# Seven half products per pair of tiles: products with unsummed weights a pair ahead, convolution taps and pooling sums one operation behind each product

## The chip, the core and the metric

The kernel runs on one core of one Trainium2 chip. The metric is the device time of one execution in microseconds (us). The engines are named as in the profile: PE (TensorE, matmuls; PEld its weight loads), DVE (VectorE), ACT (ScalarE), POOL (GpSimd) and SP (SyncE, which issues most DMAs). Each engine works through its own instructions in a fixed order and waits at each for what it needs from the others.

## The reference

One inference step of a small decoder trunk: a Mamba-2 (SSD) layer and a causal pooling layer, on 1024 prompt tokens and 8 x 8 sample tokens, 1088 in all, with width 1024. Cut to what this case touches:

```
zxbcdt = h @ w_in                                     # SSD layer: 1024 -> 2048 z + 4096 xbc + 32 dt
conv = conv_b + sum(xp[:, k:k + L] * conv_w[k] for k in range(4))
xbc_act = silu(conv);  B, C, xs = split of xbc_act;  y = scan over chunks of 128
out = rmsnorm_by_group(y * silu(z)) @ w_out

uz = h @ w_in                                         # pooling layer: 1024 -> 2048 u + 2048 z
win_sum = cs[off:off + L] - cs[off - w:off - w + L]   # windows 2, 4, 8, 16, by channel group
pooled = win_sum / min(w, pos + 1) - u
out = (pooled @ w_group * ch_scale * silu(z)) @ w_out
```

All arithmetic is float32. On PE each product is made of three terms of reduced precision: weights and activations are split into a high and a low half, and hi x hi, hi x lo and lo x hi are added up.

## The kernel before, in words

Channels lie on the 128 partitions and tokens along the free axis. An input projection takes a weight of 128 output channels (8 blocks of 128 inputs) and gives one output tile of 128 x 1088. The program runs through these stages: a start; twelve *front pairs* of output tiles of the SSD projection (`front_pairs`, from `FRONT`: z2 z3 z4 b5 x5 z5 b7 x7 z6 b0 x0 z7, where b and x tiles go through the convolution and z tiles through a SiLU); the scan with the other projections beside it; the output projection of the SSD layer; the input projection of the pooling layer, two pairs plainly and 14 *pooling pairs* (`fast_pairs`, p = 2 to 15, each a u tile, which is pooled, and a z tile); the group products; the output projection; the last norm.

The change touches the front pairs and the pooling pairs. Both go through `fast_run`. With the weights u and z of a pair of output tiles, each in two halves over the inputs (f and l), and the activations in halves over inputs and tokens (B11, B21, B22, and sums T1 to T4 made beforehand), the two tiles come from seven half products instead of eight. Each is named by the activations that it takes. One half product (`product`) is 24 matmuls of 128 x 272: two chunks of tokens, four blocks of inputs, three terms. Its results stay in two PSUM banks; some products add to what an earlier one left there. ACT copies banks out (`copy`, L1012; L1056 for the half tile that is not summed), DVE adds a bank to an earlier copy and writes the output (`put`, L1009).

The weights of the seven products are made by `w_sums`: POOL adds and subtracts raw halves (L948, L949, L951, L953), then `split_half` makes a high half on ACT (L174) and a low half on DVE or, for two of seven, on POOL (L176). A product's weight is made three products ahead. The halves lie in a ring of four tiles, so the high half of a product can only start when the product four before it is done. Raw weights (`wr`, 512 KB each) come by DMA in a ring of three, sums (`sw`) in a ring of two.

Behind a pair's last product (B22), `after("B22")` issues what the finished tiles need: in the front `proj_end`, which calls `conv_tile` (per tile: copies of the new convolution state on POOL, the first tap on ACT, L351, three taps for prompt and sample each on DVE, L349, then a SiLU on ACT, L352), in the pooling stage `u_pool` (state copies on POOL, L838 and L839; doublings of the window sum on DVE, L845; a correction, L850; and the difference, L852 and L854). A scheduler then sets the fixed order of every engine from the order in which the program issues the work and from its own estimates.

Of the kernel before, what the change touches and what calls it, by code (L numbers as in the profile page):

```python
# [28 lines left out]
POOLW = (3, 5)  # L29
# [68 lines left out]
class Build:  # L98
# [69 lines left out]
    def split_half(self, src):  # L168

        n = self.nsplit  # L170
        self.nsplit += 1
        t = self.wp.tile([P, 8, P], F32R, tag=("wh", "wl")[n % 2], bufs=2, name=self.name("w"))
        hi, lo = t[:, 0:4, :], t[:, 4:8, :]
        self.nc.scalar.activation(hi, src, AF.Copy)  # L174
        eng = self.nc.gpsimd if n % 7 in POOLW else self.nc.vector
        eng.tensor_tensor(out=lo, in0=src, in1=hi.bitcast(F32), op=ALU.subtract)  # L176
        return hi, lo
# [158 lines left out]
    def conv_tile(self, ti, raw, dst, ncv, scan):  # L336
# [6 lines left out]
        if not scan:  # L343
            w = [self.vec[:, V_CW + 4 * ti + k:V_CW + 4 * ti + k + 1] for k in range(4)]
            sd = dst[:, NP:TOK].rearrange("p (b i) -> p b i", i=8)
            for k in range(4):
                for d, r in ((dst[:, :NP], raw[:, k:k + NP]), (sd, rv[:, :, k:k + 8])):
                    if k:
                        nc.vector.scalar_tensor_tensor(out=d, in0=r, scalar=w[k], in1=d, op0=ALU.mult, op1=ALU.add)  # L349
                    else:  # L350
                        nc.scalar.activation(d, r, AF.Identity, bias=self.vec[:, V_CB + ti:V_CB + ti + 1], scale=w[0])  # L351
            nc.scalar.activation(dst, dst, AF.Silu)  # L352
            return
# [26 lines left out]
    def proj_end(self, G, ii, raw, scan=False):  # L380
        dst = self.slots.get("xbc")
        self.conv_tile(G["ti"][ii], raw, dst, G["ncv"][:, ii], scan)
# [33 lines left out]
    def proj_evict(self, G, ii, raw, ps, c):  # L416
# [3 lines left out]
        if pn < n:  # L420
            nc.scalar.activation(raw[:, 1027:1115].rearrange("p (b w) -> p b w", w=11)[:, :, 3:11],
                                 ps[:, pn:n].rearrange("p (b i) -> p b i", i=8), AF.Identity)
            self.proj_end(G, ii, raw, True)
# [409 lines left out]
    def u_pool(self, p, U):  # L833
# [8 lines left out]
        while step < w:  # L842
# [5 lines left out]
            s, step = d, 2 * step  # L848
        o = 16 - w
# [86 lines left out]
    def w_sums(self, n):  # L936
# [4 lines left out]
        u = self.stream_next_raw()  # L941
        self.stream_raw(self.wpos)
        yield self.split_half(u[:, f])
        for i in range(n):
            z = self.stream_next_raw()
            self.stream_raw(self.wpos)
            s = self.tp.tile([P, 8, P], F32, tag="sw", bufs=2, name=self.name("sw"))
            nc.gpsimd.tensor_tensor(out=s[:, f], in0=z[:, f], in1=z[:, l], op=ALU.add)  # L948
            nc.gpsimd.tensor_tensor(out=s[:, l], in0=s[:, f], in1=u[:, f], op=ALU.subtract)  # L949
            yield self.split_half(s[:, l])  # L950
            nc.gpsimd.tensor_tensor(out=z[:, f], in0=u[:, f], in1=z[:, f], op=ALU.subtract)  # L951
            yield self.split_half(z[:, f])
            nc.gpsimd.tensor_tensor(out=s[:, l], in0=u[:, l], in1=s[:, l], op=ALU.subtract)  # L953
            yield self.split_half(u[:, l])
            yield self.split_half(s[:, f])
            if i + 1 < n:
                u = self.stream_next_raw()
                self.stream_raw(self.wpos)
                yield self.split_half(u[:, f])
            yield self.split_half(z[:, l])  # L960
            yield self.split_half(s[:, l])

    def fast_init(self, n):

        self.nsplit = 0
# [8 lines left out]
    def product(self, ps, x, more=False):  # L974
# [10 lines left out]
        for c in range(2):  # L985
            t = slice(QUART * c, QUART * c + QUART)
            for k, (xh, xl) in enumerate(self.X[x]):
                nc.tensor.matmul(ps[c], hi[:, k], xh[:, t], start=(k == 0 and not more), stop=False, skip_group_check=True)  # L988
                nc.tensor.matmul(ps[c], hi[:, k], xl[:, t], start=False, stop=False, skip_group_check=True)  # L989
                nc.tensor.matmul(ps[c], lo[:, k], xh[:, t], start=False, stop=(k == 3), skip_group_check=True)  # L990

    def fast_run(self, n, make):
# [21 lines left out]
        def first(i):  # L1014
            A = banks(*(("y", "y"), ("mm", "mm"))[i % 2])
            product(A, "B11")
            s = self.tp.tile([P, HALF], F32, tag="mt2", bufs=self.nmt2, name=self.name("m1"))
            for c in range(2):
                copy(s[:, cs[c]], A[c])
            return A, s  # L1020

        A, s = first(0)
        for i in range(n):
            u, z, after = make(i)
            after("B11")
# [5 lines left out]
            E = banks("mm", "S")  # L1031
            product(E, "T3")
            v = self.tp.tile([P, HALF], F32, tag="mt2", bufs=self.nmt2, name=self.name("m7"))
            for c in range(2):
                copy(v[:, cs[c]], E[c])
            after("T3")
            B = banks("tr", "tr")
            product(B, "B21")
            for c in range(2):
                put(u, 0, c, B[c], s[:, cs[c]])  # L1040
            after("B21")
# [5 lines left out]
            nxt = first(i + 1) if i + 1 < n else None  # L1047
            product(E, "T4", True)
            for c in range(2):
                put(z, 0, c, E[c], z1[:, cs[c]])  # L1050
                after(f"z0{c}")
            after("T4")
            product(A, "B22", True)
            for c in range(2):
                for o, w in parts(u, 1, c):
                    nc.scalar.activation(o, w(A[c]), u[3])  # L1056
            after("B22")
            if nxt:
                A, s = nxt

    def fast_pairs(self, late):
# [5 lines left out]
        def make(i):  # L1067
# [3 lines left out]
            def after(x):  # L1071
# [11 lines left out]
                elif x == "B22":  # L1083
                    if p - PLAIN < len(late):
                        self.u_pool(p - PLAIN, late[p - PLAIN])
                    if p < 15:
                        self.u_pool(p, U)
# [3 lines left out]

        self.fast_run(16 - PLAIN, make)
        self.free_acts(self.hn[4:])
# [347 lines left out]
    def front_pairs(self, ops, dt):  # L1441
# [4 lines left out]

        def make(n):
# [11 lines left out]
            def after(x):  # L1459
# [9 lines left out]
                if kind != "z" and x == "B22":  # L1469
                    for i in range(2):  # L1470
                        self.proj_end(G, ii + i, ts[i])
                        if g:
                            t = G["out"].pop()
                            nc.sync.dma_start(self.xbd[g][ii + i], t)
                            sl.free(t)
                if n == 0 and x in ("B11", "T2"):
# [13 lines left out]
        self.fast_run(len(FRONT), make)  # L1490
        sl.free(*[self.T[4, k] for k in range(4)])
# [115 lines left out]
    def pool_layer(self):  # L1607
# [28 lines left out]
        for gi in range(4):  # L1636
            acts, zs = self.group_split(gi > 0), self.gin[1]
            if gi == 0:
                self.u_pool(15, U)
# [202 lines left out]
```

## Time and profile before

| | |
|---|---|
| median of 3 runs | 1648.8 us (1647.14 to 1650.06) |
| profiled execution | 1648.84 us, span 1647.1 us |
| PE busy | 1602.4 us (97%) |
| DVE busy | 1208.0 us (73%) |
| ACT busy | 860.7 us (52%) |
| POOL busy | 482.0 us (29%) |
| front pairs | 96.6 to 369 us of the span |
| pooling pairs | 1069 to 1369.4 us of the span |

In rows of the profile a group is written as line, engine, operation, output<-inputs, shapes and count; then busy time and the mean of one in ns; then the idle time of the engine just before them and who ended it. `st` is a bank of a half product, `w` a split weight, `hh`, `hl` and `t` activations, `xbc` a tile behind the convolution, `raw` one ahead of it, `u`, `ws` and `pl` the tile, its window sums and its pooled result, `pz` a z tile of the pooling layer. Rows of the timeline start with the start in us from the span's start and the duration in us; a row with x9 stands for nine instructions in a row of which the first has the shape shown. Rows of windows give the stretch, its length, the busy time (and count) of the engines, then the granted clock of PE, the DMA share and GB/s.

### The profile page before, as it was taken

How to read it: one execution, taken by the hardware profiler on the slowest of the kernel's cores; microseconds unless marked ns; L12 is line 12 of the kernel's file. 1: busy time of each engine (PE TensorE's matmuls, PEld its weight loads, DVE VectorE, ACT ScalarE, POOL GpSimd, SP SyncE). 2: the span in 40 equal slices, each digit the busy share in tenths (PEclk: the TensorE clock that was granted, in tenths of full speed). 3: DMA queues.
4: the chain of work that ended last, by engine and by line, in shares of the span. 5: the costliest groups of instructions: out<-in, count | busy, mean ns of one | idle time of the engine just before them, and what ended most of it. 6: DMA issues, size and time to landing. Idle time of an engine off the chain costs nothing.

```text
span 1647.1 us, 30656 instructions
## 1 busy us (share of the span) xinstructions
PE 1602.4 (97%) x12061; PEld 1525.9 (93%) x12061; DVE 1208.0 (73%) x1912; ACT 860.7 (52%) x1735; POOL 482.0 (29%) x527
## 2 busy tenths in 40 slices
PE   8999999999999999999999999999999999999997
PEld 6899999999888998898989899999999999999997
DVE  6863657576787878889878867966777647577886
ACT  6663445457766676675545536644333344233364
POOL 0224444331212212020211212455565640000241
PEclk9999999999999999999999999999999999999999
DMA  9422332235545555578788633033233359655783
GB/s 343 161 73 92 106 109 81 87 131 186 176 144 192 162 163 164 186 230 295 277 326 302 219 127 118 29 110 125 104 98 110 128 169 369 214 154 179 161 177 116
DMA packets 122305, 275.59 MB, mean 167 GB/s; under 512 B 18192, under 2 KB 59312, under 8 KB 122160
## 3 DMA queue, kind: packets, MB, share of 16 engines
q1 hardware_dynamic: 118128, 260.91, 45.9%
q0 software_dynamic: 4032, 12.72, 4.4%
q8 instruction: 95, 1.56, 0.4%
q14 instruction: 50, 0.41, 0.1%
HBM read 201.12 MB, written 70.23 MB: 165 GB/s over the span
## 4 chain that ended last, share of the span: by engine, by line
PE 74%; DVE 9%; DMA 5%; issue 4%; POOL 4%; ACT 3%; SPq 0%; DVEq 0%; POOLq 0%; ACTq 0%
PE mm L182 10%; PE mm L183 9%; PE mm L184 9%; PE st L990 9%; PE st L988 9%; PE st L989 9%; DVE xbc L349 3%; PE op L1229 2%; PE op L1230 2%; PE op L1228 2%; DMA acb<-acd 2%; PE y L609 2%; PE S L588 2%; PE y L613 1%; PE am L253 1%
## 5 line engine op out<-in xcount | busy, mean ns | idle before, releaser
L990 PE MATMUL st<-hh,w 128*128 128x272 f32 x832 | 243.3, 292 | 13.3 <-DVE w L176 11.8
L988 PE MATMUL st<-hh,w 128*128 128x272 f32 x832 | 241.8, 291 | 2.4 <-ACT pz L862 2.4
L989 PE MATMUL st<-hl,w 128*128 128x272 f32 x832 | 241.8, 291 | 0.0
L990 PE MATMUL st<-t,w 128*128 128x272 f32 x624 | 179.6, 288 | 0.0
L988 PE MATMUL st<-t,w 128*128 128x272 f32 x624 | 179.5, 288 | 0.0
L989 PE MATMUL st<-t,w 128*128 128x272 f32 x624 | 179.2, 287 | 0.0
L182 PE MATMUL mm<-hh,wh 128*128 128x368 f32 (+1 forms) x528 | 178.1, 337 | 0.1
L184 PE MATMUL mm<-hh,wl 128*128 128x368 f32 (+1 forms) x528 | 173.4, 328 | 0.0
L183 PE MATMUL mm<-hl,wh 128*128 128x368 f32 (+1 forms) x528 | 173.3, 328 | 0.0
L990 PEld LDWEIGHTS st<-hh,w 128*128 128x128 f32 x832 | 158.5, 190 | 15.5 <-DVE w L176 12.9
L988 PEld LDWEIGHTS st<-hh,w 128*128 128x128 f32 x832 | 158.6, 191 | 3.0 <-ACT pz L862 2.7
L989 PEld LDWEIGHTS st<-hl,w 128*128 128x128 f32 x832 | 158.6, 191 | 0.0
L596 POOL TENSOR_TENSOR hd<-h,cd 128x256 f32<-128x256 f32 x56 | 48.2, 861 | 347.5 <-DVE h L597 189.9
L1228 PE MATMUL op<-b,w 128*128 128x272 f32 x448 | 129.4, 289 | 0.0
L1229 PE MATMUL op<-b,w 128*128 128x272 f32 x448 | 128.8, 287 | 0.6 <-DVE b L1158 0.6
L182 PE MATMUL mm<-gh,wh 128*128 128x368 f32 (+1 forms) x384 | 129.1, 338 | 0.1
L1230 PE MATMUL op<-b,w 128*128 128x272 f32 x448 | 128.9, 288 | 0.0
L183 PE MATMUL mm<-gl,wh 128*128 128x368 f32 (+1 forms) x384 | 126.0, 328 | 2.4 <-DVE gl L743 2.3
L184 PE MATMUL mm<-gh,wl 128*128 128x368 f32 (+1 forms) x384 | 126.0, 328 | 0.0
L988 PEld LDWEIGHTS st<-t,w 128*128 128x128 f32 x624 | 117.6, 188 | 0.1
L990 PEld LDWEIGHTS st<-t,w 128*128 128x128 f32 x624 | 117.4, 188 | 0.0
L989 PEld LDWEIGHTS st<-t,w 128*128 128x128 f32 x624 | 117.2, 188 | 0.0
(299 smaller groups left out, 4513.0 us busy)
## 6 DMA issues: line engine op xcount, KB each, us to landing
wr<-win SPq DMA_DIRECT2D x48, 512.0 KB, 3.6
acb<-acd SPq DMA_DIRECT2D x64, 256.0 KB, 4.3
wr<-pin SPq DMA_DIRECT2D x32, 512.0 KB, 4.2
wr<-pout SPq DMA_DIRECT2D x28, 512.0 KB, 4.2
x<-x1d SPq DMA_DIRECT2D x24, 544.0 KB, 6.1
x1d<-x SPq DMA_DIRECT2D x22, 544.0 KB, 5.0
wr<-pout POOLq DMA_DIRECT2D x20, 512.0 KB, 5.5
x<-xT SPq DMA_DIRECT2D x16, 544.0 KB, 6.5
```

Source lines behind the costliest of these rows:

```text
L182: nc.tensor.matmul(ps[:, :n], hi[:, k, :], ah[:, a:a + n], start=first, stop=False)
L183: nc.tensor.matmul(ps[:, :n], hi[:, k, :], al[:, a:a + n], start=False, stop=False)
L184: nc.tensor.matmul(ps[:, :n], lo[:, k, :], ah[:, a:a + n], start=False, stop=last)
L349: nc.vector.scalar_tensor_tensor(out=d, in0=r, scalar=w[k], in1=d, op0=ALU.mult, op1=ALU.add)
L588: nc.tensor.matmul(S[:, 256 * i:256 * i + 256], Bt, xde.rearrange("p r q -> p (r q)"), start=True, stop=True)
L596: nc.gpsimd.tensor_tensor(out=hd, in0=h[-1], in1=cd.unsqueeze(2).to_broadcast([P, 4, 64]), op=ALU.mult)
L988: nc.tensor.matmul(ps[c], hi[:, k], xh[:, t], start=(k == 0 and not more), stop=False, skip_group_check=True)
L989: nc.tensor.matmul(ps[c], hi[:, k], xl[:, t], start=False, stop=False, skip_group_check=True)
L990: nc.tensor.matmul(ps[c], lo[:, k], xh[:, t], start=False, stop=(k == 3), skip_group_check=True)
L1228: nc.tensor.matmul(ps[:, :QUART], hi[:, k], xh, start=k == 0, stop=False)
L1229: nc.tensor.matmul(ps[:, :QUART], hi[:, k], xl, start=False, stop=False)
L1230: nc.tensor.matmul(ps[:, :QUART], lo[:, k], xh, start=False, stop=k == 7)
```

## The change

Four things change, all within `fast_run`, `w_sums` and what is issued behind the products.

1. Order of the products. Before, a pair ran T2, T3, B21, T1, B11 of the next pair, T4, B22. Now B11 and B21 of the next pair, whose weights are the unsummed halves of u, run ahead (`first`), and a turn of the loop is T3, B22 of the pair before, T2, B11 and B21 of the next pair, T1, T4. B22 of the last pair runs at the end.
2. Banks. B11, T2, T1 and B22 share two banks as before. T3 and T4, which had two of their own, now share theirs with B21, which had two others; the two kinds of sets alternate from pair to pair.
3. Weight sums. The four sums are other combinations (u_f - z_f; z_l less that; z_f + z_l; u_l less the second), the last of them is split for the B22 of the pair before, and it is the two unsummed halves of u that POOL splits, rather than those at two places of seven.
4. Work behind. `conv_tile` and `u_pool` are generators that yield after each tap or doubling. They go into a list `bg`, and `behind`, called at the end of each product, advances them by as many steps as the list has members. What is left is issued at the end of the stage. The two u tiles of the plain pairs are pooled in this way from the start of the pooling stage.

No product, sum, tap or doubling is added or dropped. In the new file the lines are split L175 and L173, sums L951, L952, L953 and L958, taps L348, matmuls L997 to L999, `put` L1027, `copy` L1030, the other eviction L1050, pooling L847 to L857.

```
     def w_sums(self, n):
...
+        u, last = self.stream_next_raw(), None
+        z = self.stream_next_raw()
         self.stream_raw(self.wpos)
+        yield self.split_half(u[:, f], True)
+        yield self.split_half(u[:, l])
         for i in range(n):
...
+            nc.gpsimd.tensor_tensor(out=s[:, f], in0=u[:, f], in1=z[:, f], op=ALU.subtract)
+            nc.gpsimd.tensor_tensor(out=s[:, l], in0=z[:, l], in1=s[:, f], op=ALU.subtract)
+            nc.gpsimd.tensor_tensor(out=z[:, f], in0=z[:, f], in1=z[:, l], op=ALU.add)
+            yield self.split_half(s[:, f])
+            if i:
+                yield self.split_half(last)
             yield self.split_half(s[:, l])
+            nc.gpsimd.tensor_tensor(out=s[:, f], in0=u[:, l], in1=s[:, l], op=ALU.subtract)
+            last = s[:, f]
             if i + 1 < n:
                 u = self.stream_next_raw()
+                yield self.split_half(u[:, f], True)
+                yield self.split_half(u[:, l], True)
                 self.stream_raw(self.wpos)
+            yield self.split_half(z[:, f])
             yield self.split_half(z[:, l])
+            if i + 1 < n:
+                z = self.stream_next_raw()
+                self.stream_raw(self.wpos)
+        yield self.split_half(last)
...
+        self.behind(len(self.bg))
+
+    def behind(self, n=1):
+
+        while self.bg and n:
+            if next(self.bg[0], self) is self:
+                self.bg.pop(0)
+            else:
+                n -= 1
...
+        cur, prev = first(0), None
         for i in range(n):
+            A, X, s, v, u, z, after = cur
+            product(X, "T3")
...
+            if prev:
+                finish(*prev)
...
             product(A, "T2", True)
...
+            prev = cur
+            cur = first(i + 1) if i + 1 < n else None
             product(A, "T1", True)
...
+            product(X, "T4", True)
...
+        finish(*prev)
...
                 elif x == "B22":
-                    if p - PLAIN < len(late):
-                        self.u_pool(p - PLAIN, late[p - PLAIN])
                     if p < 15:
-                        self.u_pool(p, U)
+                        self.bg.append(self.u_pool(p, U))
...
                 if kind != "z" and x == "B22":
-                    for i in range(2):
-                        self.proj_end(G, ii + i, ts[i])
...
+                    self.bg.append(ends(G, g, ii, ts))
```

How the order on the engines moves is shown at two places. First DVE behind the pair b5 of the front, whose two tiles are convolved. `w` is a low half of a weight, `raw` and `xbc` a tile ahead of and behind the convolution, the rows of L349 (L348 now) its taps, those of L1009 (L1027) results being added. Before:

```order
L176 TENSOR_TENSOR w_1988<-wr_1857,w_1988 128x512
L1009 TENSOR_TENSOR raw_1823<-st_1855,raw_1823 128x272
L1009 TENSOR_TENSOR raw_1823<-st_1856,raw_1823 128x272
L349 SCALAR_TENSOR_TENSOR xbc_2061<-raw_1823,vec,xbc_2061 128x1024 x3
L349 SCALAR_TENSOR_TENSOR xbc_2048<-raw_1820,vec,xbc_2048 128x1024
L349 SCALAR_TENSOR_TENSOR xbc_2048<-raw_1820,vec,xbc_2048 128x64
L349 SCALAR_TENSOR_TENSOR xbc_2048<-raw_1820,vec,xbc_2048 128x1024
L349 SCALAR_TENSOR_TENSOR xbc_2048<-raw_1820,vec,xbc_2048 128x64
L349 SCALAR_TENSOR_TENSOR xbc_2048<-raw_1820,vec,xbc_2048 128x1024
L349 SCALAR_TENSOR_TENSOR xbc_2048<-raw_1820,vec,xbc_2048 128x64
L176 TENSOR_TENSOR w_2080<-sw_1954,w_2080 128x512
L176 TENSOR_TENSOR w_2145<-wr_1857,w_2145 128x512
```

After, at the same place:

```order
L1027 TENSOR_TENSOR raw_1691<-st_1684,raw_1691 128x272
L348 SCALAR_TENSOR_TENSOR xbc_2251<-raw_1691,vec,xbc_2251 128x1024 x3
L175 TENSOR_TENSOR w_2109<-wr_1881,w_2109 128x512
L348 SCALAR_TENSOR_TENSOR xbc_2136<-raw_1688,vec,xbc_2136 128x1024
L348 SCALAR_TENSOR_TENSOR xbc_2136<-raw_1688,vec,xbc_2136 128x64
L348 SCALAR_TENSOR_TENSOR xbc_2136<-raw_1688,vec,xbc_2136 128x1024
L175 TENSOR_TENSOR w_2153<-wr_1881,w_2153 128x512
L348 SCALAR_TENSOR_TENSOR xbc_2136<-raw_1688,vec,xbc_2136 128x64
L348 SCALAR_TENSOR_TENSOR xbc_2136<-raw_1688,vec,xbc_2136 128x1024
L175 TENSOR_TENSOR w_2190<-sw_2186,w_2190 128x512
L348 SCALAR_TENSOR_TENSOR xbc_2136<-raw_1688,vec,xbc_2136 128x64
L1027 TENSOR_TENSOR z_2149<-st_2147,m_2151 128x272
```

The nine taps that stood together are now in blocks of three, three, two and one, with a split between each; the last row, which empties a bank of the next pair's B21, stands behind all of them.

Second POOL at the same pair: `sw` and `wr` rows are weight sums, `w` rows low halves, `ncv` rows copies of the new convolution state. Before:

```order
L948 TENSOR_TENSOR sw_1954<-wr_1857 128x512
L949 TENSOR_TENSOR sw_1954<-sw_1954,wr_1719 128x512
L951 TENSOR_TENSOR wr_1857<-wr_1719,wr_1857 128x512
L176 TENSOR_TENSOR w_1859<-wr_1719,w_1859 128x512
L341 COPY ncv_1819<-raw_1823 128x3
L342 COPY ncv_1819<-raw_1823 128x24
L953 TENSOR_TENSOR sw_1954<-wr_1719,sw_1954 128x512
L176 TENSOR_TENSOR w_2018<-wr_1719,w_2018 128x512
```

After:

```order
L951 TENSOR_TENSOR sw_2186<-wr_1953,wr_2107 128x512
L952 TENSOR_TENSOR sw_2186<-wr_2107,sw_2186 128x512
L953 TENSOR_TENSOR wr_2107<-wr_2107 128x512
L340 COPY ncv_1687<-raw_1691 128x3
L341 COPY ncv_1687<-raw_1691 128x24
L175 TENSOR_TENSOR w_2048<-wr_1953,w_2048 128x512
L175 TENSOR_TENSOR w_2077<-wr_1953,w_2077 128x512
L377 MEMSET raw_2401 128x3
L378 COPY raw_2401<-scv_2398 128x8x3
L340 COPY ncv_1687<-raw_1688 128x3
L341 COPY ncv_1687<-raw_1688 128x24
L958 TENSOR_TENSOR sw_2186<-wr_1953,sw_2186 128x512
```

Both low halves now stand together behind three sums, and the fourth sum, which overwrites what `w_2190` on DVE still reads, closes the pair.

93 lines of the change are left out of this document (41 added, 52 removed).

## The prediction

> **What bounds the kernel now.** I read the busy shares first, then the two stages that the change touches by windows, then PE's gaps there, then the engines that PE waits for. On the page:
>
> ```profile
> PE 1602.4 (97%) x12061; PEld 1525.9 (93%) x12061; DVE 1208.0 (73%) x1912; ACT 860.7 (52%) x1735; POOL 482.0 (29%) x527
> L990 PE MATMUL st<-hh,w 128*128 128x272 f32 x832 | 243.3, 292 | 13.3 <-DVE w L176 11.8
> L988 PE MATMUL st<-hh,w 128*128 128x272 f32 x832 | 241.8, 291 | 2.4 <-ACT pz L862 2.4
> ```
>
> PE is the bound and does the same matmuls in both kernels, so only its idle and slow stretches can go. The windows (length, PE busy, PEld, DVE, ACT, POOL, granted clock) of the front pairs and of the pooling pairs:
>
> ```profile
> 96.60:369.00 272.40, 260.61 (x2037) 258.37 (x2036) 161.93 (x230) 129.16 (x249) 116.64 (x118) 0.98 0.28 98
> 1069.00:1369.40 300.40, 296.45 (x2353) 295.13 (x2352) 201.76 (x245) 123.59 (x262) 163.93 (x135) 1.00 0.39 129
> ```
>
> In an undisturbed stretch of the timeline the 48 matmuls from 189.75 to 195.64 issue every 5.89/47 = 0.1253 us; the first two rows below are the first and last of them, the next the gap that follows, the last the final gap of the front's five (the other three lie between them, at 223.62, 268.52 and 293.97):
>
> ```profile
> 189.75 0.29 PE L990 MATMUL st<-t,w 128*128 128x272 f32 x1
> 195.64 0.29 PE L989 MATMUL st<-hl,w 128*128 128x272 f32 x1
> 198.47 0.59 PE L990 MATMUL st<-hh,w 128*128 128x272 f32 x1 [2.54 <-DVE w L176]
> ...
> 339.18 0.40 PE L990 MATMUL st<-hh,w 128*128 128x272 f32 x1 [1.53 <-DVE w L176]
> ```
>
> A product is 24 matmuls, 3.0 us; a pair of output tiles is seven, 21.05 us. At 0.1253 us the front's 2037 matmuls need 255.2 us, so 17.2 us are lost there; the pooling stage's 2353 need 294.8, so 5.6 are lost. Together 22.8 us: 1648.84 - 22.8 = 1626 is the floor of what this change can reach.
>
> Of the front's 17.2 us, 11.8 are PE idle for a low half of a weight (L176 on DVE), and some 0.8 go with these five restarts. The rest is clock. Windows with PE alone (length, busy, clock):
>
> ```profile
> 198.50:202.50 4.00, 4.00 (x22) 0.64 0.69 228
> 270.00:274.00 4.00, 4.00 (x23) 0.61 0.74 254
> 294.00:298.00 4.00, 4.00 (x21) 0.63 0.72 216
> ```
>
> A full-speed window of 4 us holds 32 matmuls; 30 are missing, 3.8 us, and the edges make it some 4.6. Three of five gaps are followed by such a stretch. The Trainium skill ("TensorE: Matmul & The Clock Gate", section "What's actually happening") has the clock drop after an idle window of about 3.4 us; by that rule no gap here would do it, and these rows differ: gaps with 2.6 us idle sufficed. I go by the rows, so any new gap of that size may cost half as much again.
>
> Why the split is late is seen on DVE:
>
> ```profile
> 185.56 12.25 DVE L349 SCALAR_TENSOR_TENSOR xbc<-raw,vec,xbc 128x1024 f32<-128x1024 f32 x9 [1.42 <-ACT xbc L351]
> 197.73 0.68 DVE L176 TENSOR_TENSOR w<-sw,w 128x512 fp32r<-128x512 f32 x1
> ```
>
> Nine taps stand in one block ahead of the split that PE waits for at 198.47. Part of their length is POOL. Below, a tap while POOL has nothing, two taps of which the second starts at 189.40 beside weight sums, those sums, a short tap and a sum undisturbed:
>
> ```profile
> 186.88 1.28 DVE L349 SCALAR_TENSOR_TENSOR xbc<-raw,vec,xbc 128x1024 f32<-128x1024 f32 x1
> 188.20 3.52 DVE L349 SCALAR_TENSOR_TENSOR xbc<-raw,vec,xbc 128x1024 f32<-128x1024 f32 x2
> 189.15 1.49 POOL L948 TENSOR_TENSOR sw<-wr 128x512 f32<-128x512 f32 x1 [0.79 <-DMA wr<-win]
> 190.72 2.15 POOL L949 TENSOR_TENSOR sw<-sw,wr 128x512 f32<-128x512 f32 x1
> 205.71 0.28 DVE L349 SCALAR_TENSOR_TENSOR xbc<-raw,vec,xbc 128x64 f32<-128x64 f32 x1
> 204.30 1.29 POOL L953 TENSOR_TENSOR sw<-wr,sw 128x512 f32<-128x512 f32 x1 [0.71 <-DVE w L176]
> ```
>
> A tap is 1.28 us alone and 3.52 - 1.28 = 2.24 beside a sum; a sum is 1.29 alone and 2.15 beside a tap. The two take turns.
>
> **The change, part by part.** *Taps one operation behind each product.* In the order of the new kernel the longest run of DVE work ahead of a split in a front pair is three long taps, 3 x 1.28 = 3.9 us alone; with POOL taking turns 3 x 2.24 = 6.7. A split's high half starts when the product four before it ends, so it has 9 us less its own 0.63 (below) and 0.68. The rows under it are a conv tile's first tap and its last activation, which stay on ACT:
>
> ```profile
> L174 ACT ACTIVATE w<-wr 128x512 fp32r<-128x512 f32 x47 | 29.3, 626 | 23.6 <-PE st L990 23.6
> L351 ACT ACTIVATE xbc<-raw,vec 128x1024 f32<-128x1024 f32 x12 | 14.9, 1238 | 0.0
> L352 ACT ACTIVATE xbc<-xbc 128x1088 f32<-128x1088 f32 x12 | 13.4, 1114 | 21.7 <-DVE xbc L349 21.3
> ```
>
> That is 7.7 us of room against 3.9 to 6.7. All five gaps go, and with them the half clock: -17.2. Bounds: nothing gained, or all of it; I take all, since even the contended block fits.
>
> *New sums and products ahead.* POOL now makes three sums, then the low halves of both unsummed weights, then the fourth sum, which must wait for the low half of T3's weight (DVE), and the next weight's DMA waits for the fourth sum (its buffer). This is a chain from pair to pair. Its DMA, by the front's issues (KB, us to landing):
>
> ```profile
> wr<-win SPq DMA_DIRECT2D x23, 512.0 KB, 3.6
> ```
>
> Take T as the start of T3. Without taps, the low half of the next T3's weight is ready at T+13.3 (B11 ends at T+12, plus 0.63 and 0.68), the sum at T+14.6, the weight at T+18.2, three sums at T+22.1, the first low half at T+23.4; B11 needs it at T+30. Room 6.6. In a pair with taps, DVE first passes 11 taps (6 x 1.28 + 5 x 0.28 = 9.1) and two splits from T+2.1 on (after T4's emptying and the first tap, 1.24 on ACT), so the split is done near T+13.3 alone and, after 3.4 us of POOL's work between and some idle, about T+17: the room shrinks to 3. Six of 12 front pairs have taps, in twos. In the second of two, POOL's sums meet the first three taps and take turns: 3.9 us become about 7.5. There the low half is 1 to 2 us late. Two places (after b5/x5 and b7/x7; the third two end the stage): +3.0, between 0 and 6. What is late next in that case is B11's third matmul, at the same line as now.
>
> The work that both engines must do by turns in such a pair: 6 x 1.28 + 6 x 0.28 taps, 5 x 0.68 splits, 6 x 1.29 sums and halves on POOL, some 1.4 for eight small copies: 21.9 us against 21.05 of PE. The Trainium skill ("SBUF — State Buffer", section "SBUF: two separate sides") says that a GpSimd operation and a VectorE operation with two SBUF inputs lock each other out for whole instructions; the rows above agree. By that rule each of the six pairs would lose at least 0.9, 5.4 in place of my 3.0; I stay with 3.0 because pairs without taps leave some 10 us to catch up in.
>
> *Bank shared by B21 and T3.* T3 writes the banks that DVE empties after B21. In the pairs after the first, T1 and T4 lie between, so the emptying has 6 us: cost 0 with DVE at most some 5 us behind. At the start of the front nine matmuls of T2 stand between: +0.5 (0 to 1). The transposes of the dt phase now share their banks with X of the second pair and are spread over 17 matmuls (2.1 us) where they had 28 (3.5 us); eight copies must empty them, six like the row below and two of 0.19, some 2.2 us with the way there and back: +1.0 (0 to 2).
>
> ```profile
> L494 DVE COPY tkx<-tr 128x128 f32<-128x128 f32 x4 | 1.1, 292 | 1.0 <-PE tr L493 0.9
> ```
>
> *Front end.* Taps of x0 now end late in the last pair: 9.1 us of them, the splits and emptyings between, and the second tile's first tap (1.24 on ACT) give some T+15.3; its last activation (1.11) ends by T+16.8, and the scan's first transposes come at T+18. Cost 0; with DVE 3 us later, some +2.
>
> Front: -17.2 + 3.0 + 0.5 + 1.0 = -12.7.
>
> *Pooling stage.* Its gaps are these, the first, the second and the last; three like the last stand at 1235.55, 1257.17 and 1278.79:
>
> ```profile
> 1073.06 0.40 PE L988 MATMUL st<-hh,w 128*128 128x272 f32 x1 [2.43 <-ACT pz L862]
> ...
> 1108.56 0.39 PE L990 MATMUL st<-hh,w 128*128 128x272 f32 x1 [0.35 <-POOL w L176]
> ...
> 1300.42 0.39 PE L990 MATMUL st<-hh,w 128*128 128x272 f32 x1 [0.30 <-POOL u L822]
> ```
>
> The first is 2.6 us (2.43 and its restart), the other five some 0.6 each, 3.0. At the first, DVE is full (below), and now a pooling sum of 1.4 us stands ahead as well; B21 and T3 of the first pair follow each other on one pair of banks, and both halves wait for DVE, 0.9 and 1.4: 2.3 in place of 2.6 (0 to 4.6).
>
> ```profile
> 1070.63 2.62 DVE L908 TENSOR_TENSOR hl<-x,hh 128x544 fp32r<-128x544 f32 x4
> ...
> 1247.16 6.28 DVE L845 TENSOR_TENSOR ws<-ws 128x1220 f32<-128x1220 f32 x3
> ```
> ```profile
> 1249.80 2.36 POOL L949 TENSOR_TENSOR sw<-sw,wr 128x512 f32<-128x512 f32 x1
> 1252.12 2.45 POOL L951 TENSOR_TENSOR wr<-wr,wr 128x512 f32<-128x512 f32 x1
> 1254.53 0.10 POOL L822 MEMSET u<- 128x15 f32 x1
> 1254.57 0.32 POOL L823 COPY u<-spl 128x120 f32<-128x120 f32 x1
> 1254.85 2.26 POOL L176 TENSOR_TENSOR w<-wr,w 128x512 fp32r<-128x512 f32 x1
> ```
>
> In the window-16 pairs the three doublings (6.28) and POOL's sums (2.4 each instead of 1.29) now fall together and make the half of 1254.85 late. After the change the doublings run from about T+7 on, in steps, and the sums land between T-1 and T+5: they part, and the five gaps shrink to +0.5 in all (0 to 4). At the stage's end the last splits are done at T+17.8 and T+19.0 for T+18.5 and T+19.5: +0.5 (0 to 3). Pooling: -5.6 + 2.3 + 0.5 + 0.5 = -2.3.
>
> Sum: 1648.84 - 12.7 - 2.3 = 1633.8, say 1634. The profiled execution stands at the median (1648.8), so nothing is to be added.
>
> **Rivals.** *POOL's chain becomes the bound* in all ten loaded pairs (six with taps, four of window 16). For it: 21.9 us of turns against 21.05, and its chain already sets 21.6 us per pair at window 16. Against it: the 6.6 us of room elsewhere. At 1 to 1.9 us each in place of my 3.5 in all: 1648.8 - 22.8 + 4.3 + (10 to 19) = 1640 to 1649, likeliest 1644.
>
> *Slower: T3 waits for B21's bank.* The emptying stands behind the last tap on DVE. If DVE passes that tap later than T+20.1 (my estimate is T+17 to T+18.5), PE waits at T3 in each of the six tap pairs. A wait like today's 2.8 us and half of a half-clock stretch, 4.3 in all, six times is 26: 1648.8 - 22.8 + 4.3 + 26 = 1656. It decides against the change from 3.1 us a pair on. For it: the loaded DVE and POOL; against it: two splits in the same queue would be late before.
>
> *Nothing moves*: the taps' blocks of 6.7 us and the new waits cancel, within 0.2%.
>
> **Chances.** Forecast (1626 to 1640) 0.57; chain 0.2, of which 0.02 within 0.2%; nothing moves 0.05; slower 0.18. A measurement of this kernel tells 0.2%, 3.3 us, from no change. Faster 0.57 + 0.18 = 0.75; within 0.02 + 0.05 = 0.07; slower 0.18. The range 1626 to 1647 runs from the floor to the end of most chain cases and leaves out the slower rival and about 0.02 below.
>
> **What would show it.** Front window: right if it is near 260 us with no idle for a DVE split (L175 in the new file), clock 1.00 throughout, and what is left stands at B11 after a POOL half (L175) in the pairs after x5 and x7; the DVE row of taps never longer than 7 us. Pooling window near 298 us, its first gap still there, none at window 16. The forecast is wrong if PE idles at T3 for DVE L1027 (the slow rival), if POOL's half of the unsummed weight is waited for in every pair (the chain), if half-clock stretches remain, or if the scan's first transposes wait for the activation of x0 by more than 3 us.

## The result

The changed kernel takes 1634.35 us (median of 5 runs, 1631.14 to 1639.27) against 1648.8 (median of 5 runs, 1641.25 to 1650.06): 0.9923 of the time before, 95% interval 0.9894 to 0.9952. The time is where it was forecast (1634), but it is not made up as forecast. First the page of the changed kernel, shares and the groups of half products:

```profile
PE 1598.2 (98%) x12061; PEld 1521.7 (93%) x12061; DVE 1170.1 (72%) x1914; ACT 862.5 (53%) x1737; POOL 443.0 (27%) x525
...
L999 PE MATMUL st<-hh,w 128*128 128x272 f32 x832 | 240.4, 289 | 1.9 <-POOL w L175 1.9
L997 PE MATMUL st<-hh,w 128*128 128x272 f32 x832 | 240.2, 289 | 0.0
L998 PE MATMUL st<-hl,w 128*128 128x272 f32 x832 | 239.6, 288 | 0.0
L997 PE MATMUL st<-t,w 128*128 128x272 f32 x624 | 181.5, 291 | 3.9 <-DVE z L1027 2.1
L998 PE MATMUL st<-t,w 128*128 128x272 f32 x624 | 180.8, 290 | 0.7 <-DVE t L911 0.7
```

The 11.8 us of waits for DVE halves and the 2.4 for ACT's `pz` are gone. In their place stand 1.9 for halves that POOL makes, and 3.9 + 0.7 at products that start with a `t` operand, which are new. DVE and POOL do nearly the same work (the low halves of two weights have moved from POOL to DVE) in 38 and 39 us less busy time, because they get into each other's way less: the 36 long taps of the front take 1472 ns on average where they took 1687, and of POOL's sums and halves between 1050 and 1372 us two take over 1.9 us where 26 did. The stages, by windows (length, PE, PEld, DVE, ACT, POOL, clock):

```profile
95.80:358.50 262.70, 257.93 (x2037) 255.87 (x2036) 154.68 (x233) 129.40 (x252) 106.45 (x117) 0.99 0.30 102
358.50:1054.00 695.50, 686.42 (x5113) 628.82 (x5112) 569.59 (x959) 435.73 (x979) 145.43 (x210) 1.00 0.59 196
1054.00:1353.80 299.80, 297.33 (x2354) 296.47 (x2353) 170.54 (x247) 123.56 (x261) 134.57 (x132) 0.99 0.37 129
1353.80:1632.60 278.80, 267.98 (x1938) 266.04 (x1936) 204.23 (x345) 113.10 (x158) 44.74 (x55) 0.99 0.66 188
```

From first to last half product the front takes 262.6 us (272.3 before, -9.7), the scan stage with the output projection 695.5 (700.0, -4.5), the pooling pairs 299.7 (300.4, -0.7); the start is 0.8 shorter and what follows 1.2 longer. Together -14.5. These stage times come from the starts of PE's half products in one profiled execution of each kernel, here and in the table further down.

What PE waits for in the two stages, by the timeline (every gap of 0.4 us and more, and a shorter one between the last four):

```profile
105.26 0.54 PE L997 MATMUL st<-t,w 128*128 128x272 f32 x1 [2.07 <-DVE z L1027]
...
144.90 0.33 PE L495 MATMUL tr<-kc,raw 128*128 128x128 f32 x1 [0.75 <-DVE z L1027]
...
221.75 0.39 PE L999 MATMUL st<-hh,w 128*128 128x272 f32 x1 [0.76 <-POOL w L175]
...
286.38 0.40 PE L999 MATMUL st<-hh,w 128*128 128x272 f32 x1 [1.19 <-POOL w L175]
...
1060.63 0.39 PE L997 MATMUL st<-t,w 128*128 128x272 f32 x1 [0.42 <-DVE u L1027]
1062.19 0.39 PE L997 MATMUL st<-t,w 128*128 128x272 f32 x1 [0.17 <-ACT t L910]
1063.24 0.40 PE L998 MATMUL st<-t,w 128*128 128x272 f32 x1 [0.66 <-DVE t L911]
1064.99 0.60 PE L997 MATMUL st<-t,w 128*128 128x272 f32 x1 [1.23 <-DVE u L1027]
```

The first is T3 of the first front pair, which waits for the banks that B21 has just filled; the second the transposes of the dt phase; the third and fourth B11 behind x5 and x7; the last four the start of the pooling stage. After the first and after the last the clock falls (windows: length, PE, clock, DMA share, GB/s):

```profile
102.00:109.00 7.00, 4.93 (x27) 0.76 0.23 75
1060.00:1068.50 8.50, 6.03 (x31) 0.80 0.50 171
```

Counted from start to start of the matmuls, beyond 0.1253 us each, the first stretch loses 3.9 us (2.2 in the gap, 1.6 at half clock behind it), the second 4.8 (3.4 in the four gaps, 1.4 at half clock).

### The profile page after: what moved, and what is told of

Its sections match the earlier page's. It is cut to its first block, busy times and chain, and to the rows that moved or that the text cites. A ratio compares the mean times of both kernels' runs of the same rounds, so it can differ in the third digit from the quotient of the medians.

```text
span 1632.6 us, 30674 instructions
## 1 busy us (share of the span) xinstructions
PE 1598.2 (98%) x12061; PEld 1521.7 (93%) x12061; DVE 1170.1 (72%) x1914; ACT 862.5 (53%) x1737; POOL 443.0 (27%) x525
## 5 line engine op out<-in xcount | busy, mean ns | idle before, releaser
L999 PE MATMUL st<-hh,w 128*128 128x272 f32 x832 | 240.4, 289 | 1.9 <-POOL w L175 1.9
L997 PE MATMUL st<-hh,w 128*128 128x272 f32 x832 | 240.2, 289 | 0.0
L997 PE MATMUL st<-t,w 128*128 128x272 f32 x624 | 181.5, 291 | 3.9 <-DVE z L1027 2.1
L999 PE MATMUL st<-t,w 128*128 128x272 f32 x624 | 181.1, 290 | 0.0
L999 PEld LDWEIGHTS st<-hh,w 128*128 128x128 f32 x832 | 156.5, 188 | 2.4 <-POOL w L175 2.4
L997 PEld LDWEIGHTS st<-hh,w 128*128 128x128 f32 x832 | 156.6, 188 | 0.1
L997 PEld LDWEIGHTS st<-t,w 128*128 128x128 f32 x624 | 119.1, 191 | 4.8 <-DVE z L1027 2.3
L998 PEld LDWEIGHTS st<-t,w 128*128 128x128 f32 x624 | 118.6, 190 | 1.0 <-DVE t L911 0.9
L999 PEld LDWEIGHTS st<-t,w 128*128 128x128 f32 x624 | 118.7, 190 | 0.0
```

## The experiments

Eight further kernels ran beside the kernel before, and three kernels ran once more. The edits are against the changed kernel unless said. A kernel with "one run" has no interval, and its stages come from that run.

| kernel | front | scan stage | pooling | ratio to before (95%) |
|---|---|---|---|---|
| before | 272.3 | 700.0 | 300.4 | 1 |
| changed | 262.6 | 695.5 | 299.7 | 0.9923 (0.9894 to 0.9952) |
| order without work behind | 265.3 | 697.0 | 301.5 | 0.9952 (0.9937 to 0.9966) |
| work behind without order | 255.0 | 699.6 | 300.9 | 0.9879 (0.9862 to 0.9896) |
| changed, half of u_f on DVE | 257.1 | 693.8 | 296.9 | 0.9872 (0.9848 to 0.9896) |
| changed, first B21 in own banks | 258.6 | 697.5 | 297.2 | 0.9882 (0.9865 to 0.9898) |
| changed, no taps in front | 259.1 | 696.2 | 298.4 | one run |
| changed, three repairs | 256.5 | 696.3 | 297.5 | 0.9856 (0.9836 to 0.9876) |
| work behind, other banks, late pooling | 255.0 | 698.0 | 299.5 | 0.9861 (0.9840 to 0.9881) |
| work behind, late pooling | 255.3 | 700.3 | 299.7 | one run |
| changed, once more | 262.4 | 695.5 | 301.6 | 0.9910 (0.9875 to 0.9945) |
| work behind without order, once more | 255.0 | 701.0 | 299.7 | 0.9874 (0.9843 to 0.9905) |
| changed, three repairs, once more | 256.4 | 695.1 | 299.7 | 0.9875 (0.9840 to 0.9910) |

### Which part carries the gain

Order, banks and sums, with the work behind a pair issued at once:

```
-                        self.bg.append(self.u_pool(p, U))
+                        for _ in self.u_pool(p, U):
+                            pass
...
-                    self.bg.append(ends(G, g, ii, ts))
+                    for _ in ends(G, g, ii, ts):
+                        pass
```

> New order, banks and weight sums, but the taps of a pair and its pooling sums are issued at once behind B22, as before. My theory (the taps one operation behind each product carry the gain): DVE has its block of nine taps of 12 us or more back ahead of the splits, so PE waits for a DVE half (L175) in most of the six pairs with taps, 0.5 to 3 us each, and the front takes 268 to 274 us against 262.6 in the changed kernel and 272.3 before; the whole 1640 to 1648 us. Rival (the order and the choice of the halves that POOL splits carry the gain, since a split is now needed later after the block): no waits for DVE halves, front 260 to 264, the whole 1631 to 1637 us.

The kernel before with the generators, `behind` and `bg`, but its own order of products, banks and sums:

```
+        self.behind(len(self.bg))
...
-                    if p - PLAIN < len(late):
-                        self.u_pool(p - PLAIN, late[p - PLAIN])
                     if p < 15:
-                        self.u_pool(p, U)
+                        self.bg.append(self.u_pool(p, U))
...
+        self.bg = [self.u_pool(p, t) for p, t in enumerate(late)]
```

> The kernel before with the taps and pooling sums advanced one operation behind each product, and nothing else. My theory: the five waits for DVE halves at L990 of before go here too, with the half clock behind them; the waits that the new order brings (2.2 us and half clock at the front's start, about 1 us at the dt transposes, two waits for POOL's half) are absent, so the front takes 256 to 260 us, shorter than in the changed kernel; the pooling stage keeps its first gap of 2.6 us; the whole 1626 to 1634 us. Rival (the order is needed as well): at least three waits of over 1 us for DVE halves stay, front over 265, the whole over 1637 us.

The order alone came out between my theory and the rival, at 1642.12 us and a front of 265.3. Its waits in the front, and DVE ahead of the first of them:

```profile
L999 PE MATMUL st<-hh,w 128*128 128x272 f32 x384 | 111.4, 290 | 5.5 <-DVE w L175 3.1 <-POOL w L175 2.4
```
```profile
192.58 4.84 DVE L348 SCALAR_TENSOR_TENSOR xbc<-raw,vec,xbc 128x1024 f32<-128x1024 f32 x3 [1.31 <-ACT xbc L350]
200.10 4.26 DVE L348 SCALAR_TENSOR_TENSOR xbc<-raw,vec,xbc 128x1024 f32<-128x1024 f32 x6 [2.69 <-ACT xbc L350]
204.28 1.29 DVE L175 TENSOR_TENSOR w<-wr,w 128x512 fp32r<-128x512 f32 x2
```

The block of taps is back ahead of the splits, with 2.69 us in it in which DVE waits for ACT's first tap of the second tile. PE waits 3.1 us for DVE in place of 11.8: at three places in place of five, 1.0 to 1.1 us each, and no half clock follows. At the first of them PE's wait began 11.4 us after the start of the block, where at 198.47 in the kernel before it was 10.4, so the split is needed a microsecond later after the block. Whether the order of the products or the choice of the halves that POOL splits makes this microsecond, no run parts. So the order does gain something by itself in the front, some 7 us; that I had denied. At the start of its pooling stage one wait of 3.8 us for the bank and the half clock behind it cost 6.7 us.

The work behind alone gains more than the whole change: 1630.29 us. Its front, a window without a gap, and its pooling stage:

```profile
96.50:351.70 255.20, 255.20 (x2037) 1.00 0.32 103
1051.20:1352.30 301.10, 297.97 (x2355) 0.99 0.40 130
```

2037 matmuls at 0.1253 us are 255.2 us: nothing is left to gain in the front. The rival's three waits for DVE halves are not there. DVE at the place where PE had waited at 198.47:

```profile
185.52 2.61 DVE L349 SCALAR_TENSOR_TENSOR xbc<-raw,vec,xbc 128x1024 f32<-128x1024 f32 x2 [1.42 <-ACT xbc L351]
188.04 0.69 DVE L176 TENSOR_TENSOR w<-sw,w 128x512 fp32r<-128x512 f32 x1
188.65 9.43 DVE L349 SCALAR_TENSOR_TENSOR xbc<-raw,vec,xbc 128x1024 f32<-128x1024 f32 x6
198.00 0.68 DVE L176 TENSOR_TENSOR w<-wr,w 128x512 fp32r<-128x512 f32 x1
```

The split that had come at 197.73, behind nine taps, now comes at 188.04, behind two. Six taps still stand in one block of 9.43 us, but ahead of a split that PE needs later: by the count of splits and products it ends 3.1 us before its first use, at 201.75. So what counts is not the length of a block but which split stands behind it.

On top of this the new order removes nothing in the front and brings its own waits, 7.6 us. In the pooling stage the first gap is 3.1 us here, with half clock behind it, 6.0 us in all. The two kernels ran once more beside each other on one chip:

> The changed kernel once more, beside the two below on one chip. By the stages so far: front 262 to 263 us, pooling stage 299 to 300.5 us; the scan stage between them anywhere from 694 to 700 us, by how many of its unchanged gaps of 2 us and more are followed by half clock (none: 694 to 696, one: 696 to 700). The whole 0.990 to 0.994 of before.

> The kernel before with the work behind each product alone, once more. Front 255 to 255.5 us, pooling stage 299 to 301 us, scan stage as for the changed kernel. If the new order has a cost of its own, this one is 2 to 7 us shorter than the changed kernel: 0.986 to 0.990 of before; if the order costs nothing, the two are within 1 us.

The changed kernel took 1635.77 us (6 runs, 1632.98 to 1637.72; 0.9910 of before, 0.9875 to 0.9945), the work behind alone 1629.06 (6 runs, 1627.89 to 1631.97; 0.9874, 0.9843 to 0.9905), fronts 262.4 and 255.0. The intervals of the ratios overlap, since the kernel before spread from 1643 to 1660 in this comparison, but the runs of the two kernels do not: the new order costs some 6.7 us. Two expectations by stage were missed. The pooling stage of the changed kernel took 301.6 in place of 299 to 300.5, mostly since one more wait, 1.4 us for DVE's emptying into `pz`, stands at its end. And the scan stage of the work behind alone took 701.0, not what it takes in the changed kernel (695.5); that difference goes the other way than the cost of the order.

### The waits that the order brings

The low half of u_f, the first unsummed half of each pair, on DVE in place of POOL:

```
-        yield self.split_half(u[:, f], True)
+        yield self.split_half(u[:, f])
...
-                yield self.split_half(u[:, f], True)
+                yield self.split_half(u[:, f])
```

> The changed kernel with the low half of u_f made on DVE in place of POOL. My theory (POOL's three sums, taking turns with the taps, make this half late): the two waits of 0.8 and 1.2 us for POOL's half behind x5 and x7 go, nothing else moves by more than 0.5 us, front 260 to 261.5 us against 262.6. Rival (the whole chain over the sums and the DMA is late, whichever engine splits): waits of the same size stay at the same products, or move to the next product, whose half POOL still makes.

Both waits for POOL's half are gone, and none has moved to the half that POOL still makes. The front, at 257.1, is shorter than expected: with the half on DVE the emptying of B21's banks also stands earlier in DVE's order, and the first gap shrinks to 0.7, with no half clock behind it. What is left at the front's half products (0.8 us more stand at the dt transposes):

```profile
L997 PE MATMUL st<-t,w 128*128 128x272 f32 x288 | 83.2, 289 | 0.7 <-DVE z L1027 0.7
```

Why POOL's half was late in the changed kernel can be followed from its split to PE: DVE, then POOL, then the weight's DMA (issued at 209.25 on SP, landed at 213.07 by the last of its semaphore updates), POOL again, and DVE beside it. The row at 213.23 names an emptying on DVE as the last to end before it, but that ended only 0.14 us after the weight had landed.

```profile
207.15 0.69 DVE L175 TENSOR_TENSOR w<-sw,w 128x512 fp32r<-128x512 f32 x1
```
```profile
207.92 1.30 POOL L958 TENSOR_TENSOR sw<-wr,sw 128x512 f32<-128x512 f32 x1 [6.76 <-DVE w L175]
...
213.23 1.30 POOL L951 TENSOR_TENSOR sw<-wr,wr 128x512 f32<-128x512 f32 x1 [3.81 <-DVE raw L1027]
214.60 2.34 POOL L952 TENSOR_TENSOR sw<-wr,sw 128x512 f32<-128x512 f32 x1
216.91 2.27 POOL L953 TENSOR_TENSOR wr<-wr 128x512 f32<-128x512 f32 x1
219.13 1.18 POOL L340 COPY ncv<-raw 128x3 f32<-128x3 f32 x1
220.25 0.20 POOL L341 COPY ncv<-raw 128x24 f32<-128x24 f32 x1
220.42 2.52 POOL L175 TENSOR_TENSOR w<-wr,w 128x512 fp32r<-128x512 f32 x2
```
```profile
209.25 0.33 SPq L120 DMA_DIRECT2D wr<-win  x1
```
```profile
214.52 5.75 DVE L348 SCALAR_TENSOR_TENSOR xbc<-raw,vec,xbc 128x1024 f32<-128x1024 f32 x3 [1.31 <-ACT xbc L350]
```

Three sums take 5.9 us and three taps 5.75, where each three would take some 3.9 alone; PE goes on at 221.75, when the first of the two halves is there. Without the taps (part of the convolution is left out):

```
-                    if k:
+                    if k and self.nsplit < 0:
                         nc.vector.scalar_tensor_tensor(out=d, in0=r, scalar=w[k], in1=d, op0=ALU.mult, op1=ALU.add)
-                    else:
+                    elif not k:
```

> The changed kernel without the 72 convolution taps of the front pairs on DVE (part of the convolution is left out; ACT's first tap and all else stay). My theory (POOL's sums and DVE's taps take turns, and that makes POOL's half late): the three sums behind each DMA take 1.3 us each in place of up to 2.3, and the two waits of 0.8 and 1.2 us for POOL's half go; front 260 to 261.5 us. Rival (the chain of fourth sum, DMA and sums is too long by itself): the waits stay.

Both waits are gone, and the front is 3.5 us shorter, more than expected: 2.5 us are the two waits, and 0.8 the wait at the dt transposes, which shrank too. The first of the sums takes 1.70 us in place of the 1.3 expected, the other two 1.30. The sums at the same place:

```profile
208.84 1.70 POOL L951 TENSOR_TENSOR sw<-wr,wr 128x512 f32<-128x512 f32 x1 [3.82 <-DMA wr<-win]
210.62 1.30 POOL L952 TENSOR_TENSOR sw<-wr,sw 128x512 f32<-128x512 f32 x1
211.88 1.30 POOL L953 TENSOR_TENSOR wr<-wr 128x512 f32<-128x512 f32 x1
```

The chain itself starts earlier too (the sum that frees the buffer at 203.73 in place of 207.92, against a front that starts at the same time), so the taps make it late twice: they hold up the split ahead of it, and they take turns with the sums. The run does not part the two.

The bank of the first B21:

```
-            product(X, "B21")
+            Y = X if i else banks("tr", "tr")
+            product(Y, "B21")
             for c in range(2):
-                put(u, 0, c, X[c], s[:, cs[c]])
+                put(u, 0, c, Y[c], s[:, cs[c]])
```

> The changed kernel with B21 of the first pair of each stage in banks of its own, so that T3 does not wait for DVE to empty them. My theory (the shared bank makes the gap of 2.1 us at the front's start, and the half clock behind it follows from the gap): both gone, front about 3.5 us shorter, 259 us; in the pooling stage the two waits for DVE u (0.4 and 1.2 us) go and those for T3's operand (0.2 and 0.7 us) stay or grow by up to 1. Rival (T3's operand is as late as the bank): the gap stays at over 1 us with another releaser.

The gap at the front's start is gone with the half clock behind it, and the front is 4.0 us shorter (258.6). The two waits for POOL's half stay:

```profile
L999 PE MATMUL st<-hh,w 128*128 128x272 f32 x384 | 111.2, 290 | 1.8 <-POOL w L175 1.8
```

In the changed kernel DVE had four operand splits ahead of that emptying:

```profile
100.27 4.59 DVE L1431 TENSOR_TENSOR hl<-x,hh 128x544 fp32r<-128x544 f32 x4
104.78 0.78 DVE L1027 TENSOR_TENSOR z<-st,m 128x272 f32<-128x272 f32 x2
```

In the pooling stage the bank's waits went too, and those for T3's operand stayed, at 0.9 and 0.5, with no half clock behind them: 2.0 us lost at its start where the changed kernel loses 4.8.

### The start of the pooling stage

All three repairs in one: the half on DVE, the bank, and the two late u tiles pooled from T3 of the first pair on.

```
-        self.bg = [self.u_pool(p, t) for p, t in enumerate(late)]
...
+                elif p == PLAIN and x == "T3":
+                    self.bg += [self.u_pool(q, t) for q, t in enumerate(late)]
```

> The changed kernel with the low half of u_f on DVE, B21 of the first pair in its own banks, and the two late u tiles pooled only from T3 of the first pooling pair on. If each cause found so far stands alone, the gains add: front 255.5 to 257 us (the wait at the dt transposes, about 1 us, stays), pooling stage 295 to 297 us, the whole 1621 to 1628 us. If DVE, which takes on 26 halves, becomes the bound in the pairs with taps, waits for DVE halves of 0.5 us and more appear there and the whole stays at 1628 to 1634 us.

The gains add in the front (256.5), DVE does not become the bound, and the whole takes 1627.12 us. The pooling stage, at 297.5, is just past what was expected and no shorter than with the half on DVE (296.9) or the bank (297.2) alone, so pooling the two late tiles later brought nothing that shows. At the pooling stage's start one gap stays, for T3's operand:

```profile
1058.57 0.39 PE L998 MATMUL st<-t,w 128*128 128x272 f32 x1 [2.14 <-DVE t L911]
```

The same start with the order of before, first in other banks and then in its own:

```
-            A = banks(*(("y", "y"), ("mm", "mm"))[i % 2])
+            A = banks(*(("mm", "mm"), ("y", "y"))[i % 2])
```

> The order and the sums of before, with the taps and pooling sums one operation behind each product, the first pair of a stage in the mm banks in place of the y banks, and the two late u tiles pooled only from T3 of the first pooling pair on. My theory (work behind carries the gain, the new order is not needed, and the 3.1 us wait at the pooling stage's start is that for ACT to empty the y bank of the last plain tile): front 255 to 256 us, pooling stage 295 to 298 us, the whole 1621 to 1628 us. Rival (the start of the pooling stage waits for the operands that DVE and ACT split, whatever the bank): a gap of 2 us or more stays there, pooling stage over 299 us, the whole 1627 to 1633 us.

> As the kernel with work behind alone, but with the two late u tiles pooled only from T3 of the first pooling pair on; the banks stay y first. If DVE's load there (two pooling sums of 1.4 us and a correction of 1.3 ahead of the operand splits) holds ACT, which then empties the y bank late: the 3.1 us wait at the start of the pooling stage shrinks to 0 to 1 us, pooling stage 295 to 297.5. If it is ACT's own queue, it stays at 2 to 3 us.

With the other banks the wait for `pz` is gone and another has its place; without them it stays, whatever DVE has ahead:

```profile
1055.55 0.59 PE L992 MATMUL st<-t,w 128*128 128x272 f32 x1 [2.34 <-ACT m L1025]
```
```profile
1055.66 0.39 PE L992 MATMUL st<-hh,w 128*128 128x272 f32 x1 [3.04 <-ACT pz L866]
```

So both expectations of a free start were wrong: with the other banks the pooling stage took 299.5 us and the whole 1629.08, as the rival had it. In every arrangement that ran PE loses 2 us and more there, for `pz`, for a bank, for a copy or for T3's operand. What is common to them is the split of the pooling layer's operands on ACT and DVE just ahead (`hh`, `hl`, `t`); that this work is the bound there is not shown, since no run changes it by itself.

The changed kernel with its three repairs ran once more beside the two above:

> The changed kernel with the three repairs, once more. Front 256 to 257 us, pooling stage 297 to 298 us: 7 to 9 us shorter than the changed kernel in these two stages, 0.984 to 0.988 of before for the whole.

It took 1628.48 us (5 runs, 1626.67 to 1632.88; 0.9875, 0.9840 to 0.9910), front 256.4, pooling stage 299.7 in place of 297 to 298: the gap for T3's operand is as long as before (2.2 us), but now 1.6 us of half clock follow it, and a wait of 0.6 us stands at the end. By these runs the best versions lie at 0.985 to 0.988 of before and cannot be told from each other.

## Why the prediction came out as it did

By its steps, in us against the profiled execution of before; the measured column is counted from start to start of PE's matmuls, beyond 0.1253 us each:

| step | forecast | measured |
|---|---|---|
| five waits for DVE halves and their half clock | -17.2 | -17.1, none left |
| two waits for POOL's half behind x5 and x7 | +3.0 | +2.5 |
| dt transposes | +1.0 | about +0.9 |
| front's start, shared bank | +0.5 | +3.9 |
| end of front | 0 | 0 |
| pooling: its start | -0.3 | +2.2 |
| pooling: five gaps at window 16 and before | -2.5 | -2.9, none left |
| pooling: end | +0.5 | 0 (+1.5 when the kernel ran once more) |
| the other stages | 0 | -4.1 |

**Right** were the term that carries the sum and its cause: with the taps in blocks of three, 6.2 us at the longest, no split on DVE is late, and the work behind alone shows that handing out the taps is enough. The comparison of a block's length with 7.7 us of room was on the safe side: in the work behind alone blocks of 9.43 us make no split late. Right too, in place, cause and nearly in size, were the two waits for POOL's half: 0.92 and 1.36 us from start to start beyond the usual 0.1253, at the third matmul of B11, as the working said, and 0.2 at the matmuls next to them. The window-16 gaps went, and POOL's sums and the doublings do part there: from 1068 us on no sum of POOL takes over 1.9 us, where they took 2.3 to 2.5. That the parting is what removes the gaps is not shown: with the work behind alone the sums still take 2.3 to 2.5 us in these pairs, and the gaps are gone as well.

**Wrong** is first the step "At the start of the front nine matmuls of T2 stand between: +0.5 (0 to 1)". I counted the matmuls between the two products, and not what DVE has to do ahead of the emptying: the 4.59 us of operand splits above. The gap is 2.2 us, and the half clock behind it makes it 3.9 in all; with that bank of its own the gap and the half clock went together. The bank rival was right about the mechanism, but at the two starts alone; in the pairs with taps DVE empties the bank in time. So two of the signs that the prediction itself had set for being wrong came true, PE idle at T3 for DVE and half-clock stretches that remain, though each at the start of a stage and not in the pairs that the prediction had in mind.

Second, the start of the pooling stage was forecast at 2.3 us lost in place of 2.6; 4.8 were measured, just past the end of my range (4.6). The working had two halves of 0.9 and 1.4 us; there were four gaps, which lose 3.4 us, and half clock behind them, 1.4, for which it had no term. With the first B21 in its own banks 2.0 are left.

Third, the scan stage was taken as unchanged. PE's order there is the same, and it took 4.5 us less. Part of that is clock: before, two stretches of half clock stand there, after gaps with 2.15 and 1.91 us idle; the changed kernel has the same two gaps, with 1.70 and 1.92 idle, and no half clock. Matmul by matmul (the same 5112 in both) these two stretches make 2.8 of the 4.5 us. Another 1.0 is a wait of 1.24 us for ACT's `Bt` at 858.41, of which the changed kernel has 0.3; the rest are smaller differences both ways. Such waits come and go within one kernel: with the work behind alone PE idles 1.06 us for this `Bt` in one profile and not at all in the other, and 1.77 and 2.43 us for the `Bt` of the first row below.

```profile
923.89 0.70 PE L588 MATMUL S<-xd,Bt 128*128 128x256 f32 x2 [2.15 <-ACT Bt L566]
...
1036.25 0.43 PE L182 MATMUL pl<-hh,wh 128*128 128x352 f32 x1 [1.91 <-ACT hh L319]
```
```profile
910.70 0.70 PE L590 MATMUL S<-xd,Bt 128*128 128x256 f32 x2 [1.70 <-ACT Bt L568]
...
1021.63 0.43 PE L181 MATMUL pl<-hh,wh 128*128 128x352 f32 x1 [1.92 <-ACT hh L318]
```

Over all profiles this stage takes 698.0 to 701.0 us in the five with the order of before and 693.8 to 697.5 in the eight with the new one. The two groups do not overlap, so the new order may well help there, through other banks or through DMAs that fall otherwise; why stays open, since no run changes that stage alone. So that the total was met to 0.4 us is luck: a gain of 4.1 us outside the two stages, which nobody forecast, made up for most of the 4.6 that the two stages gained less than forecast. By its parts the forecast for the two stages was -15.0 and the measurement -10.4.

## What to carry to other kernels

Work that is issued in one piece behind a loop's turn is late for whoever stands behind it in the queue; handed out one operation per step, the same instructions cost PE nothing here, since the split that PE needed next no longer stood behind all of them, and that alone brought this front to its floor. A reordering that lets results live in fewer banks should be judged at the start of the loop, where the producer and the next user follow each other, by what the emptying engine still has in its queue. When a total agrees with a forecast, compare the stages before believing the reasons.

## What the runs showed of the hardware

The clock falls after gaps of about 2 us, but not always. Of the twelve gaps with 2.0 to 2.7 us idle between half products in all profiles, eight were followed by half clock. The gap for `hh` near 1020 us stands in all 13 profiles at 2.23 to 2.25 us from start to start; half clock follows in 8 of them. The window behind it, in the kernel before and in the changed one:

```profile
1036.00:1040.00 4.00, 3.71 (x15) 0.71 0.02 4
```
```profile
1021.50:1025.50 4.00, 3.83 (x22) 1.00 0.02 4
```

Behind this gap the half clock costs 1.0 to 1.2 us, behind those between half products 1.4 to 1.6, so a single profile of this kernel is uncertain by that at each such gap. The Trainium skill ("TensorE: Matmul & The Clock Gate", section "What's actually happening") speaks of an idle window of about 3.4 us that runs freely. That one gap has two outcomes, 8 of 13, is what a freely running window would give; that the whole of 3.4 us must be idle does not agree with these gaps. Waits of 0.8 to 1.5 us that stood alone between half products, as for POOL's half, were never followed by half clock here.

A tap on DVE and a sum on POOL take turns: up to 2.2 and 2.3 us beside each other, 1.28 and 1.30 alone, and two sums out of three at 1.30 again once the taps were left out.
